# Low parts of the MLP weights: half of them by an adding transfer instead of a DVE subtraction

## The chip, the core and the metric

The kernel runs on one core of a Trainium2 chip, as one launch. The metric is device microseconds (us) from start to end of that launch. The engines are PE (TensorE matmul, with PEld for its weight loads), DVE (VectorE), ACT (ScalarE), POOL (GpSimd) and SP (SyncE, which here only issues transfers); transfers of all queues run on the core's 16 DMA engines.

## What is computed

A decoder trunk of two layers over 256 tokens of width 2048, all in float32: layer 0 mixes with a gated DeltaNet, layer 1 with differential attention; each layer then has an MLP and a gated per-layer embedding (PLE), and a final RMSNorm closes. The change touches only the MLP, whose hidden width is 8192, and the buffers of the final norm.

```python
hn = rmsnorm(h, norm_mlp[i])
h = h + jnp.square(jax.nn.relu(hn @ mlp_w1[i])) @ mlp_w2[i]
gate = jax.nn.sigmoid(rmsnorm(h, norm_ple[i]) @ ple_w_gate[i])
h = h + (p[i] @ ple_w_proj[i]) * gate
```

## The kernel before

Every large product is done in a split form. Both operands are float32; each is written as a high part, rounded to the matmul type fp32r, and a low part, which is the raw value minus the high part. Three matmuls then replace one: high by high, high by low, low by high (L150 to L152 in `g2`, L166 to L168 in `g1`).

Weights come in by `chunk` (L117): SP loads 1 MB of raw weights into a tile `raw` of 128 partitions by 2048 float32 (L122; three buffers, pool `wraw`). The tile is split into two halves of 1024 columns. For each half ACT casts `whi` from `raw` (L131), and DVE writes `wlo` = `raw` - `whi` (L132). `whi` and `wlo` have three buffers each (pool `whl`), so a cast for half n+3 waits until PE has read half n. A half feeds 24 matmuls of 256 columns in `g2` or 12 matmuls of 512 columns in `g1`.

The MLP (`mlp`, L553 on) works through the hidden width in four quarters q. `first(q)` multiplies the normalised input by `mlp_w1` with `g2`: four blocks `nb` of 512 columns with four chunks each. At the end of a block ACT applies relu (L574), DVE squares (L575), ACT casts the high part `hidh` (L578) and DVE subtracts for the low part `hidl` (L579). `second(q)` multiplies by `mlp_w2` with `g1`, again four blocks of four chunks, and DVE adds the result to the stream `h` (L587). The order is first 0, first 1, second 0, first 2, second 1, first 3, second 2, second 3. Each stage has 16 chunks, so one MLP has 128 chunks, and the two MLPs have 256 chunks, 512 halves.

Each engine works through its own queue in order, and a queue stands still while its next instruction waits. The scheduler of the language sets the order of instructions on each queue when the program is built; semaphores tie the queues together. A new load of `raw` waits until all readers of that buffer's earlier contents are done.

The layer's tiles come from a pool `ffn0` or `ffn1` with two buffers for each name: `hidh`, `hidl`, `relu` and others. `ple` loads its `p` tiles from POOL's queue (L600). `final` (L723) loads `final_norm` into a `hidl` buffer from POOL's queue (L725) and writes its results into eight tiles `y`.

Of the kernel before, what the change touches and what calls it, by code (L numbers as in the profile page):

```python
# [10 lines left out]
F32 = mybir.dt.float32  # L11
F32R = mybir.dt.float32r
AF = mybir.ActivationFunctionType
ALU = mybir.AluOpType
AX = mybir.AxisListType

P = 128
D = 2048
T = 256
NT = T // P  # L20
KD = D // P
# [16 lines left out]
class Trunk:  # L38
# [75 lines left out]
        self.w_gdn = self.cols[:, 112:113]  # L114
        self.w_sub = self.cols[:, 113:115]

    def chunk(self, src, kn, cols):  # L117

        nc = self.nc
        raw = self.wraw.tile([P, 2048], F32, name="raw")  # L120
        size = kn * cols
        nc.sync.dma_start(out=raw[:, :size].rearrange("p (k n) -> p k n", k=kn),  # L122
                          in_=src.rearrange("(k p) n -> p k n", p=P))
        res = []
        step = 1024 // cols
        for k0 in range(0, kn, step):
            kk = min(step, kn - k0)
            sl = raw[:, k0 * cols:(k0 + kk) * cols]
            hi = self.whl.tile([P, 1024], F32R, name="whi")[:, :kk * cols]
            lo = self.whl.tile([P, 1024], F32R, name="wlo")[:, :kk * cols]  # L130
            nc.scalar.copy(hi, sl)  # L131
            nc.vector.tensor_tensor(lo, sl, hi.bitcast(F32), ALU.subtract)  # L132
            res.append((hi.rearrange("p (k n) -> p k n", k=kk),
                        lo.rearrange("p (k n) -> p k n", k=kk), k0, kk))
        return res

    def g2(self, x, w, nk, c0, cols, kn):

        nc = self.nc
        xh, xl = x  # L140
        nct = cols // P
        banks = [self.bank() for _ in range((nct + 1) // 2)]
        for kb in range(0, nk, kn):
            for hi, lo, k0, kk in self.chunk(w[kb * P:(kb + kn) * P, c0:c0 + cols], kn, cols):
                for k in range(kk):
                    kt = kb + k0 + k
                    for ct in range(nct):
                        o = banks[ct // 2][:, (ct % 2) * T:(ct % 2) * T + T]
                        cs = slice(ct * P, ct * P + P)
                        nc.tensor.matmul(o, hi[:, k, cs], xh[:, kt], start=kt == 0 and ct % 2 == 0, stop=False, skip_group_check=True)  # L150
                        nc.tensor.matmul(o, hi[:, k, cs], xl[:, kt], start=False, stop=False, skip_group_check=True)  # L151
                        nc.tensor.matmul(o, lo[:, k, cs], xh[:, kt], start=False, stop=kt == nk - 1, skip_group_check=True)  # L152
        return banks

    def g1(self, x, w, nk, c0, kn=4, pool=None):

        nc = self.nc
        xh, xl = x
        banks = [self.bank(512, pool) for _ in range(NT)]
        for kb in range(0, nk, kn):  # L160
            for hi, lo, k0, kk in self.chunk(w[kb * P:(kb + kn) * P, c0:c0 + 512], kn, 512):
                for k in range(kk):
                    kt = kb + k0 + k
                    for t in range(NT):
                        ts = slice(t * P, t * P + P)
                        nc.tensor.matmul(banks[t], xh[:, kt, ts], hi[:, k], start=kt == 0, stop=False)  # L166
                        nc.tensor.matmul(banks[t], xh[:, kt, ts], lo[:, k], start=False, stop=False)  # L167
                        nc.tensor.matmul(banks[t], xl[:, kt, ts], hi[:, k], start=False, stop=kt == nk - 1)  # L168
        return banks
# [388 lines left out]
    def mlp(self, h, layer, w, pool):  # L558
        nc, d = self.nc, self.d
        w1, w2 = d["mlp_w1"][layer], d["mlp_w2"][layer]  # L560
        self.transposed(h, [(self.xa, w)])
        r = self.rstd(h)
        r2 = self.small.tile([P, NT], F32, name="r2")
        nc.vector.tensor_tensor(r2, r, r, ALU.mult)

        def first(q):
            hh = pool.tile([P, KD, T], F32R, name="hidh")
            hl = pool.tile([P, KD, T], F32R, name="hidl")
            for nb in range(4):
                for b, bk in enumerate(self.g2(self.xa, w1, KD, q * D + nb * 512, 512, 4)):  # L570
                    k = nb * 4 + 2 * b
                    a = pool.tile([P, 512], F32, name="relu")
                    s = pool.tile([P, 512], F32, name="relu2")
                    nc.scalar.activation(a, bk, AF.Relu)  # L574
                    nc.vector.tensor_tensor(s, a, a, ALU.mult)  # L575
                    fh = hh[:, k:k + 2].rearrange("p a b -> p (a b)")
                    fl = hl[:, k:k + 2].rearrange("p a b -> p (a b)")
                    nc.scalar.copy(fh, s)  # L578
                    nc.vector.tensor_tensor(fl, s, fh.bitcast(F32), ALU.subtract)  # L579
            return hh, hl  # L580

        def second(q, hid):
            for nb in range(4):
                bk = self.g1(hid, w2[q * D:(q + 1) * D], KD, nb * 512)
                for t in range(NT):
                    s = h[t][nb]
                    nc.vector.scalar_tensor_tensor(s, bk[t], r2[:, t:t + 1], s, ALU.mult, ALU.add)  # L587

        prev = first(0)
        for q in range(1, 4):  # L590
            cur = first(q)
            second(q - 1, prev)
            prev = cur
        second(3, prev)

    def ple(self, h, layer, w, pool):
# [125 lines left out]
    def final(self, h, pool):  # L722
        nc = self.nc  # L723
        fw = pool.tile([P, D], F32, name="hidl")
        nc.gpsimd.dma_start(out=fw, in_=self.d["final_norm"].partition_broadcast(P))  # L725
        y = [[pool.tile([P, 512], F32, name=f"y{t}{b}", bufs=1) for b in range(4)] for t in range(NT)]
        for b in range(4):
            for t in range(NT):
                nc.vector.tensor_tensor(y[t][b], h[t][b], fw[:, b * 512:(b + 1) * 512], ALU.mult)
        r = self.rstd(h)  # L730
        for t in range(NT):
            for b in range(4):
                if b % 2 == 0:
                    nc.scalar.activation(y[t][b], y[t][b], AF.Copy, scale=r[:, t:t + 1])
                else:
                    nc.vector.tensor_scalar(y[t][b], y[t][b], r[:, t:t + 1], None, ALU.mult)
                nc.sync.dma_start(out=self.out[0, t * P:(t + 1) * P, b * 512:(b + 1) * 512], in_=y[t][b])
# [55 lines left out]
```

## Time and profile before

| what | value |
|---|---|
| median of the two runs | 2951.43 us (2949.67 and 2953.2) |
| the profiled execution: its time | 2951.79 us |
| the profiled execution: its span in the profile | 2950.0 us |
| PE busy | 2909.7 us, 99% of the span |
| DVE busy | 1782.8 us, 60% |
| ACT busy | 1451.8 us, 49% |
| POOL busy | 60.4 us, 2% |
| DMA, mean rate over the span | 179 GB/s |

The page gives busy times of one execution. Busy time of PE is the union of matmuls that overlap, so the time that a matmul costs is the distance between the starts of two neighbours, not its own duration. An arrow in a row of idle time names what the engine waited for. The share of DMA is the mean busy share of the 16 engines.

### The profile page before, as it was taken

Reading aid. Unit: us, or ns where it says so; the run is one execution under the profiler, and the core shown is the slowest. Engines: PE = TensorE matmul, PEld = TensorE weight load, DVE = VectorE, ACT = ScalarE, POOL = GpSimd, SP = SyncE. Lnnn points to the kernel's source line nnn. Section 1 sums busy time; section 2 is a strip of 40 time slices with the busy share of each in tenths; the row PEclk is TensorE's granted clock in tenths of the full one; section 3 lists DMA queues with packets and bytes.
Section 4 is the critical chain, followed back from the end, with each engine's and each line's share of the span. In section 5 each row is a group of like instructions: output and inputs, shape, how many; then the busy total and the mean of one; then the engine's idle time right before and its main releaser. Section 6 shows DMA issues by size and latency. Waiting matters only on the chain.

```text
span 2950.0 us, 44777 instructions
## 1 busy us (share of the span) xinstructions
PE 2909.7 (99%) x18730; PEld 2626.2 (89%) x18730; DVE 1782.8 (60%) x2324; ACT 1451.8 (49%) x1947; POOL 60.4 (2%) x64
## 2 busy tenths in 40 slices
PE   8999999999999999999999999999999999999998
PEld 8989889988988998989988889987899899898886
DVE  7879766666666555555555565567555555555565
ACT  5655555545545443444434553367544444344454
POOL 1011000000000000000000000000000000000000
PEclk9999999999999999999999999999999999999999
DMA  6654544455445665655565556654566565556654
GB/s 200 207 168 140 175 161 138 149 175 161 133 143 182 194 196 190 188 194 189 186 198 189 178 170 198 191 166 144 183 192 197 189 192 192 188 186 198 202 172 155
DMA packets 289595, 527.19 MB, mean 179 GB/s; under 512 B 25966, under 2 KB 44560, under 8 KB 289264
## 3 DMA queue, kind: packets, MB, share of 16 engines
q1 hardware_dynamic: 288160, 521.77, 55.3%
q8 instruction: 147, 2.41, 0.3%
q0 software_dynamic: 816, 2.03, 0.2%
q10 hardware_dynamic: 416, 0.53, 0.1%
q14 instruction: 56, 0.46, 0.0%
HBM read 520.03 MB, written 4.26 MB: 178 GB/s over the span
## 4 chain that ended last, share of the span: by engine, by line
PE 93%; DVE 4%; ACT 2%; DMA 0%; issue 0%; POOL 0%; ACTq 0%; DVEq 0%
PE accb L166 16%; PE accb L167 16%; PE accb L168 16%; PE accb L151 13%; PE accb L152 13%; PE accb L150 13%; PE misb L429 2%; DVE wlo L132 1%; ACT whi L131 1%; PE misb L434 1%; PE misb L412 0%; PE misb L444 0%; PE misb L193 0%; PE misb L421 0%; DMA h<-x 0%
## 5 line engine op out<-in xcount | busy, mean ns | idle before, releaser
L132 DVE TENSOR_TENSOR wlo<-raw,whi 128x1024 fp32r<-128x1024 f32 x970 | 1190.1, 1228 | 985.0 <-ACT whi L131 983.6
L131 ACT CAST whi<-raw 128x1024 fp32r<-128x1024 f32 x970 | 1019.2, 1051 | 1296.8 <-PE accb L168 677.5
L150 PE MATMUL accb<-xha,whi 128*128 128x256 f32 x3344 | 939.4, 281 | 0.8 <-ACT whi L131 0.8
L151 PE MATMUL accb<-xla,whi 128*128 128x256 f32 x3344 | 937.6, 280 | 1.6 <-DVE xla L198 1.6
L152 PE MATMUL accb<-xha,wlo 128*128 128x256 f32 x3344 | 936.9, 280 | 0.5 <-DVE wlo L132 0.5
L152 PEld LDWEIGHTS accb<-xha,wlo 128*128 128x128 f32 x3344 | 633.2, 189 | 0.7 <-DVE wlo L132 0.7
L151 PEld LDWEIGHTS accb<-xla,whi 128*128 128x128 f32 x3344 | 629.7, 188 | 2.4 <-DVE xla L198 2.2
L150 PEld LDWEIGHTS accb<-xha,whi 128*128 128x128 f32 x3344 | 630.4, 189 | 1.4 <-ACT whi L131 1.0
L168 PE MATMUL accb<-whi,hidl 128*128 128x512 f32 x1024 | 398.5, 389 | 0.0
L167 PE MATMUL accb<-wlo,hidh 128*128 128x512 f32 x1024 | 398.5, 389 | 0.0
L166 PE MATMUL accb<-whi,hidh 128*128 128x512 f32 x1024 | 398.5, 389 | 0.0
L166 PE MATMUL accb<-whi,xha 128*128 128x512 f32 x640 | 254.2, 398 | 1.2 <-ACT xha L197 1.2
L167 PE MATMUL accb<-wlo,xha 128*128 128x512 f32 x640 | 252.8, 395 | 0.1
L168 PE MATMUL accb<-whi,xla 128*128 128x512 f32 x640 | 251.9, 394 | 0.0
L168 PEld LDWEIGHTS accb<-whi,hidl 128*128 128x128 f32 x1024 | 192.3, 188 | 40.1
L166 PEld LDWEIGHTS accb<-whi,hidh 128*128 128x128 f32 x1024 | 192.3, 188 | 39.9
L167 PEld LDWEIGHTS accb<-wlo,hidh 128*128 128x128 f32 x1024 | 192.3, 188 | 39.1
L166 PEld LDWEIGHTS accb<-whi,xha 128*128 128x128 f32 x640 | 120.4, 188 | 26.2 <-ACT xha L197 2.5
L167 PEld LDWEIGHTS accb<-wlo,xha 128*128 128x128 f32 x640 | 120.5, 188 | 25.0 <-DVE wlo L132 1.4
L168 PEld LDWEIGHTS accb<-whi,xla 128*128 128x128 f32 x640 | 120.3, 188 | 24.2
L166 PE MATMUL accb<-whi,oh 128*128 128x512 f32 x256 | 101.1, 395 | 0.8 <-ACT oh L469 0.8
L167 PE MATMUL accb<-wlo,oh 128*128 128x512 f32 x256 | 101.1, 395 | 0.0
(276 smaller groups left out, 2616.5 us busy)
## 6 DMA issues: line engine op xcount, KB each, us to landing
raw<-mlp_w SPq DMA_DIRECT2D x256, 1024.0 KB, 5.2
raw<-gdn_w_in SPq DMA_DIRECT2D x97, 1024.0 KB, 5.1
raw<-gdn_w_out SPq DMA_DIRECT2D x32, 1024.0 KB, 5.0
raw<-ple_w_gate SPq DMA_DIRECT2D x32, 1024.0 KB, 5.0
raw<-w_kv SPq DMA_DIRECT2D x32, 1024.0 KB, 5.2
raw<-diff_w_q SPq DMA_DIRECT2D x16, 1024.0 KB, 5.0
raw<-diff_w_o SPq DMA_DIRECT2D x16, 1024.0 KB, 5.0
gcb<-gcd SPq DMA_DIRECT2D x16, 256.0 KB, 4.3
```

The costliest lines, as they stand in the source:

```text
L131: nc.scalar.copy(hi, sl)
L132: nc.vector.tensor_tensor(lo, sl, hi.bitcast(F32), ALU.subtract)
L150: nc.tensor.matmul(o, hi[:, k, cs], xh[:, kt], start=kt == 0 and ct % 2 == 0, stop=False, skip_group_check=True)
L151: nc.tensor.matmul(o, hi[:, k, cs], xl[:, kt], start=False, stop=False, skip_group_check=True)
L152: nc.tensor.matmul(o, lo[:, k, cs], xh[:, kt], start=False, stop=kt == nk - 1, skip_group_check=True)
L166: nc.tensor.matmul(banks[t], xh[:, kt, ts], hi[:, k], start=kt == 0, stop=False)
L167: nc.tensor.matmul(banks[t], xh[:, kt, ts], lo[:, k], start=False, stop=False)
L168: nc.tensor.matmul(banks[t], xl[:, kt, ts], hi[:, k], start=False, stop=kt == nk - 1)
L429: nc.tensor.matmul(ps[:, h * P:(h + 1) * P], NTt[:, 2 * h + c], X[:, h * P:(h + 1) * P], start=True, stop=True)
L434: nc.tensor.matmul(ps[:, h * P:(h + 1) * P], UB[:, 2 * h + c], X[:, h * P:(h + 1) * P], start=True, stop=True)
```

## The change

`chunk` gets an argument `pool`, which only the MLP's calls of `g2` and `g1` pass on. With it, the second half of every chunk (`k0` not 0) gets its low part in another way: ACT writes `dlo` = -`raw`, rounded to fp32r, into a tile of four new buffers, which is the negated high part; then a transfer from POOL's queue adds the raw half to it in place, from one place in SBUF to another. DVE's subtraction for that half is gone. The first half of every chunk stays as it was. All products outside the MLP stay as they were. The four buffers take 16 KB of each partition; `final` now keeps its results in one `hidh` buffer of the pool instead of eight tiles of its own.

```diff
@@ chunk
             hi = self.whl.tile([P, 1024], F32R, name="whi")[:, :kk * cols]
-            lo = self.whl.tile([P, 1024], F32R, name="wlo")[:, :kk * cols]
             nc.scalar.copy(hi, sl)
-            nc.vector.tensor_tensor(lo, sl, hi.bitcast(F32), ALU.subtract)
+            if pool and k0:
+                lo = pool.tile([P, 1024], F32R, name="dlo", bufs=4)[:, :kk * cols]
+                nc.scalar.activation(lo, sl, AF.Copy, scale=-1.0)
+                nc.gpsimd.dma_start(out=lo.bitcast(F32), in_=sl, accum_op=ALU.add)
+            else:
+                lo = self.whl.tile([P, 1024], F32R, name="wlo")[:, :kk * cols]
+                nc.vector.tensor_tensor(lo, sl, hi.bitcast(F32), ALU.subtract)
@@ mlp
-                for b, bk in enumerate(self.g2(self.xa, w1, KD, q * D + nb * 512, 512, 4)):
+                for b, bk in enumerate(self.g2(self.xa, w1, KD, q * D + nb * 512, 512, 4, pool)):
-                bk = self.g1(hid, w2[q * D:(q + 1) * D], KD, nb * 512)
+                bk = self.g1(hid, w2[q * D:(q + 1) * D], KD, nb * 512, wpool=pool)
@@ final
-        y = [[pool.tile([P, 512], F32, name=f"y{t}{b}", bufs=1) for b in range(4)] for t in range(NT)]
+        ys = pool.tile([P, 2 * D], F32, name="hidh")
+        y = [[ys[:, (4 * t + b) * 512:(4 * t + b + 1) * 512] for b in range(4)] for t in range(NT)]
```

The scheduler also moves instructions. On ACT in the first MLP, stage first 0, the queue before has for each chunk its two casts, chunk after chunk; the numbers of `raw` tell the chunks apart.

```order
L131 CAST whi_9311<-raw_9309 128x1024
L578 CAST hidh_9001<-relu2_9238 128x512
L574 ACTIVATE relu_9243<-accb_9004 128x512
L131 CAST whi_9315<-raw_9309 128x1024
L578 CAST hidh_9001<-relu2_9244 128x512
L131 CAST whi_9369<-raw_9367 128x1024
L131 CAST whi_9373<-raw_9367 128x1024
L131 CAST whi_9427<-raw_9425 128x1024
```

The same place of ACT's queue in the changed kernel, a little further on (consecutive chunks are raw_9873, raw_9932, raw_10007, raw_10066):

```order
L131 CAST whi_9875<-raw_9873 128x1024
L131 CAST whi_9879<-raw_9873 128x1024
L134 ACTIVATE dlo_10015<-raw_10007 128x1024
L131 CAST whi_9934<-raw_9932 128x1024
L131 CAST whi_9938<-raw_9932 128x1024
L134 ACTIVATE dlo_10074<-raw_10066 128x1024
L131 CAST whi_10009<-raw_10007 128x1024
L131 CAST whi_10013<-raw_10007 128x1024
```

The negated copy of a chunk stands ahead of the casts of the chunk before it: dlo_10015 of raw_10007 comes before both casts of raw_9932, so it is the first reader of its chunk.

On POOL, in the second MLP, the queue had between the loads of `p` (L606 is L600 of before) and the end only the load of `final_norm`; now the adding transfers stand there, and the load of `final_norm` is among them.

```order
L606 DMA p_26091<-p 128x256
L606 DMA p_26092<-p 128x256
L135 DMA dlo<-raw 128x1024 x115
L731 DMA hidl<-final_norm 128x2048
L135 DMA dlo<-raw 128x1024 x13
```

Thirteen adding transfers now stand behind the load of `final_norm`, which waits for a `hidl` buffer. SP's queue keeps its order.

At the entry of the first MLP the queue of ACT was, before (`xha` is the high part of the MLP's input):

```order
L131 CAST whi<-raw 128x1024 x2
L197 ACTIVATE xha<-misb,cols 128x256 x4
L178 ACTIVATE junk,ss<-h_81 128x512
L197 ACTIVATE xha<-misb,cols 128x256 x3
```

and is now, at the same place:

```order
L131 CAST whi<-raw 128x1024
L134 ACTIVATE dlo<-raw 128x1024
L203 ACTIVATE xha<-misb,cols 128x256 x7
L184 ACTIVATE junk,ss<-h_81 128x512
```

A negated copy has taken the place of the second cast ahead of `xha`; that cast follows later.

## Rows read from the trace of the kernel before

**Rows 1.** The page: span, engines, and the two costliest groups (line, engine, tiles, count | busy, mean ns).
```profile
span 2950.0 us, 44777 instructions
PE 2909.7 (99%) x18730; PEld 2626.2 (89%) x18730; DVE 1782.8 (60%) x2324; ACT 1451.8 (49%) x1947; POOL 60.4 (2%) x64
...
L132 DVE TENSOR_TENSOR wlo<-raw,whi 128x1024 fp32r<-128x1024 f32 x970 | 1190.1, 1228 | 985.0 <-ACT whi L131 983.6
L131 ACT CAST whi<-raw 128x1024 fp32r<-128x1024 f32 x970 | 1019.2, 1051 | 1296.8 <-PE accb L168 677.5
```

**Rows 2.** Busy time by stretch, stages of both MLPs (PEclk: granted clock; then DMA share, GB/s).
```profile
931.50:1102.90 171.40, 171.40 (x1515) 171.40 (x1514) 97.07 (x99) 82.75 (x97) 0.00 (x0) 1.00 0.61 191
1102.90:1189.90 87.00, 87.00 (x386) 72.07 (x385) 45.86 (x43) 35.34 (x36) 0.00 (x0) 1.00 0.60 194
1189.90:1280.40 90.50, 90.50 (x770) 90.48 (x769) 47.85 (x46) 40.44 (x45) 0.00 (x0) 1.00 0.59 187
...
sum 1401.00, PE 1401.00 PEld 1281.41 DVE 749.78 ACT 614.98 POOL 0.54; mean PE 116.75 PEld 106.78 DVE 62.48 ACT 51.25 POOL 0.04
```

**Rows 3.** Waits, first MLP, 931.5 to 1632 us (us in total, times, longest).
```profile
DVE wlo L132 <- ACT whi L131: 317.1, 254, 1.6
ACT whi L131 <- PE accb L168: 199.7, 124, 1.7
ACT whi L131 <- PE accb L151: 154.6, 98, 1.8
```

**Rows 4.** DMA of one stage, second 0, 1102 to 1190 us.
```profile
DMA packets 8452, 16.84 MB, mean 191 GB/s; under 512 B 256, under 2 KB 256, under 8 KB 8448
q1 hardware_dynamic: 8448, 16.78, 59.2%
raw<-mlp_w SPq DMA_DIRECT2D x17, 1024.0 KB, 5.0
```

**Rows 5.** DMA around the load of final_norm, 2746 to 2754 us.
```profile
q1 hardware_dynamic: 624, 1.25, 49.7%
q0 software_dynamic: 144, 1.05, 31.0%
raw<-mlp_w SPq DMA_DIRECT2D x2, 1024.0 KB, 5.1
hidl<-final_norm POOLq DMA_DIRECT2D x1, 1024.0 KB, 7.0
```

**Rows 6.** The tile raw over the whole run: its landing times.
```profile
DMA to landing us min/median/max: 3.7/5.1/9.5
```

**Rows 7.** ACT in first 2, in order of time (start, us, engine, ... [idle before]).
```profile
1209.79 1.05 ACT L131 CAST whi<-raw 128x1024 fp32r<-128x1024 f32 x1 [1.78 <-PE accb L151]
1212.02 0.60 ACT L574 ACTIVATE relu<-accb 128x512 f32<-128x512 f32 x1 [1.19 <-PE accb L152]
...
1213.57 0.62 ACT L578 CAST hidh<-relu 128x512 fp32r<-128x512 f32 x1
```

**Rows 8.** PE and DVE at the end of the last product, in order of time.
```profile
2934.27 0.39 PE L166 MATMUL misb<-whi,ph 128*128 128x512 f32 x1
2936.76 0.39 PE L168 MATMUL misb<-whi,pl 128*128 128x512 f32 x1
2936.58 1.37 DVE L619 TENSOR_TENSOR gate<-gate,misb 128x512 f32<-128x512 f32 x2 [5.24 <-PE misb L168]
```

**Rows 9.** POOL in order of time: loads of p and of final_norm.
```profile
924.82 1.13 POOL L600 DMA_DIRECT2D p<-p  x2 [145.61 <-PE misb L193]
2746.96 0.54 POOL L725 DMA_DIRECT2D hidl<-final_norm  x1 [619.51 <-DVE h L587]
```

**Rows 10.** ACT and PE at the entry of the first MLP, in order of time.
```profile
924.29 1.05 ACT L131 CAST whi<-raw 128x1024 fp32r<-128x1024 f32 x1 [1.73 <-PE accb L168]
925.24 1.56 ACT L197 ACTIVATE xha<-misb,cols 128x256 fp32r<-128x256 f32 x4
927.04 0.39 PE L151 MATMUL accb<-xla,whi 128*128 128x256 f32 x1 [0.78 <-DVE xla L198]
```

More of the change, by code (lines that the diff above doesn't have):

```diff
@@ L115, in constants2, with chunk @@
         self.w_sub = self.cols[:, 113:115]
-    def chunk(self, src, kn, cols):
+    def chunk(self, src, kn, cols, pool=None):
         nc = self.nc
@@ L135, in chunk, with g2 @@
         return res
-    def g2(self, x, w, nk, c0, cols, kn):
+    def g2(self, x, w, nk, c0, cols, kn, wpool=None):
         nc = self.nc
@@ L143, in g2 @@
         for kb in range(0, nk, kn):
-            for hi, lo, k0, kk in self.chunk(w[kb * P:(kb + kn) * P, c0:c0 + cols], kn, cols):
+            for hi, lo, k0, kk in self.chunk(w[kb * P:(kb + kn) * P, c0:c0 + cols], kn, cols, wpool):
                 for k in range(kk):
@@ L153, in g2, with g1 @@
         return banks
-    def g1(self, x, w, nk, c0, kn=4, pool=None):
+    def g1(self, x, w, nk, c0, kn=4, pool=None, wpool=None):
         nc = self.nc
@@ L160, in g1 @@
         for kb in range(0, nk, kn):
-            for hi, lo, k0, kk in self.chunk(w[kb * P:(kb + kn) * P, c0:c0 + 512], kn, 512):
+            for hi, lo, k0, kk in self.chunk(w[kb * P:(kb + kn) * P, c0:c0 + 512], kn, 512, wpool):
                 for k in range(kk):
```

## The prediction

> **What bounds the kernel now.** I read the page first: PE is busy for 2909.7 of 2950.0 us, DVE for 1782.8 and ACT for 1451.8 [rows 1]. An average over stages decides nothing, so I read the MLP's stages next: in both MLPs together PE is busy for 1401.00 of 1401.00 us, at a granted clock of 1.00, with DVE at 749.78 and ACT at 614.98 [rows 2]. The waits of that stretch say the same from the other side: DVE waits for ACT's cast (317.1 us), ACT waits for PE to give back a `whi` buffer (199.7 and 154.6 us), and no row has PE waiting for DVE [rows 3]. So the chain there is matmul after matmul, and the engine that the change relieves is two steps away from it. The tempo is one chunk per 87.00 / 16 = 5.44 us in `second` and about 5.66 us in first 2 (90.50 / 16) [rows 2]; a half takes 2.72 us.
>
> **What the change removes.** 256 subtractions of 1228 ns each [rows 1], 314 us of DVE work, all of it hidden under PE. Its worth on the end is nothing: no wait of PE goes with it.
>
> **What it adds, step by step.**
>
> ACT: 256 copies of 128x1024. The nearest row is the cast of the same shape, 1051 ns [rows 1], so 269 us. In a chunk of `second` ACT then has 3 x 1.05 = 3.15 us of 5.44; at the end of a block in `first` two relus (0.60) and two casts to `hidh` (0.62) are added once in four chunks [rows 7]. It fits, and PE covers it.
>
> POOL: 256 issues. A POOL issue takes 0.54 us [rows 9], 138 us over 1401: covered.
>
> The transfers: 256 times 512 KB, SBUF to SBUF, with an add. No row shows one, so I bound its cost from both sides. In one stage the loads of `raw` take 59.2% of the engines' time [rows 4]: 0.592 x 5.44 = 3.22 us of each engine per chunk, and 2.22 us are free. A transfer of 512 KB is 32 KB for each of 16 engines. The loads' packets of 2 KB take 0.592 x 88 x 16 / 8448 = 0.099 us each [rows 4]; the packets of `final_norm`, about 8 KB, take 0.310 x 8 x 16 / 144 = 0.276 us [rows 5]. At these prices 32 KB moved once cost 4 x 0.276 = 1.10 us or 16 x 0.099 = 1.58 us. If an add must read both its source and its target through the same engine, it is twice that, 2.20 or 3.16 us. The rows of the new transfer are 4 KB long, a third of the way from the one packet to the other: 1.26 us for one pass, 2.53 us for two. One pass gives 3.22 + 1.26 = 4.48 of 5.44 us, hidden. Two give 5.75, which is over by 0.31 us. The free 2.22 us are the point from which it decides.
>
> I take the hidden case. The nearest row is 1 MB that POOL's queue moved at the start of second 3, twice the new transfer's bytes: within 8 us, the two loads of `raw` beside it landed in 5.1 us, as without it, and it landed itself in 7.0 us [rows 5, 6]. Also, loads at 59.2% of the time carry 191 GB/s on average [rows 4], while the 8 us around `final_norm` carried (1.25 + 1.05) MB, 287 GB/s, at 49.7 + 31.0 = 80.7% [rows 5].
>
> The Trainium skill speaks against it: in "Collectives: The Full Stack", section "The bandwidth ceiling: the fold count and why AG ≠ RS ≠ AR", an add inside a transfer costs no time of its own, but it needs two source reads on the same read ring and so halves the rate. By that rule the second pass is the case, and the time is that of the first rival below. No row here shows an adding transfer, so no trace yet agrees or disagrees.
>
> **Latency of the new chain.** The order puts the negated copy of chunk c+2 behind the second cast of chunk c. That cast starts when PE has left half 2c-2; the copy ends about 2.1 us later, and PE reaches the second half of chunk c+2 six halves after it left half 2c-2, at 16.3 us. The slack is 14.2 us; a POOL-issued 1 MB landed in 7.0 us [rows 5]. With four `dlo` buffers the target is free by then. So the landing alone does not stall PE.
>
> **The new wait, and who is queued behind it.** The copy is now the first reader of its `raw` tile, and ACT's queue has the two casts of the chunk before behind it. The load of chunk c+3 starts when the second cast of chunk c is done; after the landing come copy, cast, cast of chunk c+2, and its last cast lets the next load go. This ring may take two chunks, 10.88 us. It holds 3.15 us of ACT, so a landing of up to 7.7 us costs nothing. The landing is 5.1 us in the median and 9.5 us at its longest [rows 6]; one pass beside it makes it 5.1 + 1.26 = 6.4 us, two passes 7.6 us. In the hidden case 1.3 us are left.
>
> **Moved.** On POOL thirteen transfers stand behind the load of `final_norm`, which waited until DVE's add to `h` at 2746.96 us [rows 9], the end of second 2. The first of the thirteen belongs to the fourth chunk of second 3; its copy is due some 5 us later. No stall. At the entry of each MLP a copy takes the place of a cast ahead of `xha`, where PE does wait (0.78 us) [rows 10]; the cast was over by 925.34 us, and the copy may have to wait for the pool's memory until about 924.8 us, when `p` went out [rows 9], so it ends at about 925.9: 0.6 us later, 1.2 us for both. The results of `final` in `hidh` cost nothing, since that buffer was given back by second 2.
>
> **Sum.** The profiled execution's own time is 2951.79 us, span 2950.0 and 1.8 around it; that is 0.4 us above the median of the runs. Removed 0, entry +1.2, the rest hidden: 2953.0.
>
> A bound for what I can't explain: first 0 and 1 hold 1515 matmuls in 171.40 us, 0.113 us each; first 2 holds 770 in 90.50, 0.118 us, with the same code and no wait [rows 2]. Four stages of 768 at 0.0044 us are 13.5 us that another layout could win or lose.
>
> **The rivals.**
>
> *The DMA engines become the bound (slower).* An add in two passes needs 5.75 us per chunk at the middle price: +0.31 x 256 = +79 us, 3032 us. At the price of 2 KB packets it is 3.22 + 3.16 = 6.38: +0.94 x 256 = +241 us, 3194 us. For it: nothing in the kernel moves so many bytes per chunk now, and source and target are both in SBUF. Against: the row of `final_norm` [rows 5]. It decides at 2.22 us of engine time per transfer.
>
> *ACT's queue waits for its load (slower).* If landings stretch over 7.7 us for another reason than engine time, casts come late and, round the ring, loads too. At the longest landing of the trace, 9.5 us [rows 6], the ring takes 12.65 us, 6.33 per chunk: +0.89 x 256 = +228 us, 3181 us. For it: the copy waits where the cast had a landing long behind it. Against: the median landing leaves 2.6 us.
>
> *PE gets quicker with a quieter DVE (faster).* If the slow stages fell to the tempo of first 0, 13.5 us would go: 2939 us; over 2% it would take 59 us of 1401. Against: in the last microseconds, where DVE had been idle for 5.24 us, eleven distances between 512-column matmuls take 2.49 us, 0.226 each [rows 8], the same as 87.00 / 384 = 0.227 in `second`, with DVE busy for 45.86 of 87.00 us [rows 2]. The tempo does not hang on DVE.
>
> **Chances and range.** Hidden: 0.60. DMA engines the bound: 0.25. ACT's queue: 0.11. Quicker PE: 0.04. The prediction is the likeliest, 2953 us, with a range of its own of 2936 to 2969 (the 13.5 us each way and a little for the entry). Over all cases the range is 2936 to 3195: it takes in the two-pass case at both prices and the ACT case, and leaves out longer adds and a faster PE, about 0.12. Two per cent, about what a measurement of this kernel can tell from no change, is 59 us. Within it lie the hidden case and the cheapest part of the two-pass case, 0.62; slower are the rest of the two rivals, 0.34; faster 0.04.
>
> **What the profile after should show.** DVE's subtractions fall from 970 to 714 and DVE to about 1469 us; ACT rises to about 1721, POOL to about 199. The software queue carries 134 MB more. If I am right, PE stays busy for all of both MLPs, landings of `raw` are 5 to 7 us, and the queue's share is below 41% of the MLP's time. If the first rival holds, the DMA share in the MLP is above 95% and PE waits for `dlo` or for `whi`. If the second holds, the share stays under 90%, and ACT's largest wait is a copy for the landing of `raw`. What would make me wrong above all is the engine time of an add, which no row here shows.

## The result and the profile of the changed kernel

The changed kernel takes 3021.04 us in the median (3018.29 and 3023.79) against 2951.43: ratio 1.0239, 95% interval 1.0209 to 1.0268. It is 70 us slower. The forecast of 2953 us missed, and with it the case that was given 0.60. The range to 3195 held the time because it took in the two slower rivals.

The page of the changed kernel, the lines that answer to [rows 1]; behind the span and the engines stand two DMA queues (packets, MB, share), the chain that ended last by engine and by line, and two transfers with KB each and median us to landing:

```profile
span 3022.0 us, 45900 instructions
PE 2941.2 (97%) x18730; PEld 2626.7 (87%) x18730; DVE 1473.3 (49%) x2068; ACT 1667.8 (55%) x2203; POOL 282.9 (9%) x320
...
q1 hardware_dynamic: 288160, 521.77, 51.3%
q0 software_dynamic: 37680, 136.26, 23.7%
...
PE 54%; DMA 26%; DVE 7%; ACT 7%; issue 4%; POOL 0%; ACTq 0%; SPq 0%; DVEq 0%; POOLq 0%
DMA raw<-mlp_w 25%; PE accb L173 9%; PE accb L174 8%; PE accb L172 8%; PE accb L158 7%; PE accb L156 7%; PE accb L157 7%; DVE wlo L138 5%; ACT whi L131 4%; PE misb L435 2%; DMA dlo<-raw 1%; ACT relu L580 1%; PE misb L440 1%; PE misb L418 1%; PE misb L450 0%
...
raw<-mlp_w SPq DMA_DIRECT2D x256, 1024.0 KB, 7.9
dlo<-raw POOLq DMA_DIRECT2D x256, 512.0 KB, 6.7
```

DVE lost its 310 us, ACT gained 216, the software queue 134 MB. But the loads of `raw` now land in 7.9 us, and a quarter of the chain is their landing.

Where the 72 us between the two profiled spans lie, by the starts of PE's matmuls: the two MLPs hold all of it, 29.2 us in the first (707.9 before, 737.0 now) and 42.5 in the second (707.9, 750.4); the rest sums to 0.3. By stage, first MLP and second: first 0 with first 1 +12.9 and +15.2; second 0 +4.8 and +6.3; first 2 -0.1 and -0.4; second 1 +6.0 and +5.7; first 3 0.0 and +0.3; second 2 with second 3 +5.6 and +15.5. Stretches of the changed kernel, columns as in [rows 2]: second 0, first 2, second 1:

```profile
1115.70:1207.50 91.80, 89.28 (x386) 71.39 (x385) 26.62 (x27) 49.18 (x52) 13.94 (x16) 1.00 1.00 276
1207.50:1297.90 90.40, 89.64 (x769) 89.35 (x768) 28.11 (x30) 53.40 (x60) 13.94 (x16) 1.00 1.01 278
1297.90:1390.92 93.02, 90.08 (x387) 71.23 (x385) 26.83 (x28) 49.27 (x52) 13.93 (x16) 1.00 1.00 273
```

The share of the DMA engines (last but one) went from 0.60 to 1.00. A chunk now takes 5.74 us in second 0 and 5.65 in first 2. Where PE needed 5.44 before, time is lost; first 2 and 3, which needed 5.66, lose nothing on balance. DMA of second 0 (1116 to 1207 us), as in [rows 4]:

```profile
q1 hardware_dynamic: 8429, 16.75, 51.4%
q0 software_dynamic: 2288, 8.32, 48.3%
...
raw<-mlp_w SPq DMA_DIRECT2D x16, 1024.0 KB, 8.0
dlo<-raw POOLq DMA_DIRECT2D x16, 512.0 KB, 6.6
```

An adding packet takes 0.483 x 91 x 16 / 2288 = 0.307 us. A transfer has nine packets on each engine, so 2.77 us where the sum had taken 1.26. The loads' own part fell, from 3.22 us a chunk to 0.514 x 5.74 = 2.95. The sum, 5.72 us, fills the chunk; this reads like the first rival, engines with no time left. The chain of the same stage, in order of time (start, us, what), tells of something narrower:

```profile
1122.52 7.96 DMA raw<-mlp_w
...
1130.57 0.04 ACT dlo L134
...
1130.69 0.84 issue
1131.53 1.04 ACT whi L131
...
1132.60 1.24 DVE wlo L138
1133.84 0.02 SPq L123
...
1133.90 7.67 DMA raw<-mlp_w
```

A load lands; ACT makes the negated copy of that chunk, then casts the chunk before it; DVE subtracts there; this frees a buffer, and SP starts the next load. That is 7.96 + 3.42 = 11.38 us, and the order gives it two chunks: 5.69 us each. What SP waits for in the same stage (us in total, times, longest) shows a second chain of almost the same length:

```profile
SPq L123 <- DMA dlo<-raw: 73.2, 16, 6.3
SPq L123 <- DVE wlo L138: 10.1, 16, 1.1
```

The add is also a reader of `raw`. SP waits for it first, and for DVE's subtraction 0.63 us (10.1 / 16) longer. The experiments had to tell whether the engines' time or these chains set the tempo.

### The profile page after: what moved, and what is told of

Read it like the earlier page. It is cut to its first block, busy times and chain, and to the rows that moved or that the text cites. A ratio compares the mean times of both kernels' runs of the same rounds, so it can differ in the third digit from the quotient of the medians.

```text
span 3022.0 us, 45900 instructions
## 1 busy us (share of the span) xinstructions
PE 2941.2 (97%) x18730; PEld 2626.7 (87%) x18730; DVE 1473.3 (49%) x2068; ACT 1667.8 (55%) x2203; POOL 282.9 (9%) x320
## 3 DMA queue, kind: packets, MB, share of 16 engines
q8 instruction: 147, 2.41, 0.3%
## 4 chain that ended last, share of the span: by engine, by line
PE 54%; DMA 26%; DVE 7%; ACT 7%; issue 4%; POOL 0%; ACTq 0%; SPq 0%; DVEq 0%; POOLq 0%
DMA raw<-mlp_w 25%; PE accb L173 9%; PE accb L174 8%; PE accb L172 8%; PE accb L158 7%; PE accb L156 7%; PE accb L157 7%; DVE wlo L138 5%; ACT whi L131 4%; PE misb L435 2%; DMA dlo<-raw 1%; ACT relu L580 1%; PE misb L440 1%; PE misb L418 1%; PE misb L450 0%
## 5 line engine op out<-in xcount | busy, mean ns | idle before, releaser
L138 DVE TENSOR_TENSOR wlo<-raw,whi 128x1024 fp32r<-128x1024 f32 x714 | 876.2, 1229 | 1214.3 <-ACT whi L131 1213.0
L158 PE MATMUL accb<-xha,wlo 128*128 128x256 f32 x2320 | 654.5, 282 | 10.8 <-DVE wlo L138 10.7
L134 ACT ACTIVATE dlo<-raw 128x1024 fp32r<-128x1024 f32 x256 | 271.8, 1062 | 593.4 <-DMA raw<-mlp_w 589.7
L158 PEld LDWEIGHTS accb<-xha,wlo 128*128 128x128 f32 x2320 | 440.0, 190 | 15.6 <-DVE wlo L138 15.3
L135 POOL DMA_DIRECT2D dlo<-raw x256 | 223.1, 871 | 1236.4 <-ACT dlo L134 1043.0
L158 PE MATMUL accb<-xha,dlo 128*128 128x256 f32 x1024 | 285.3, 279 | 5.8 <-DMA dlo<-raw 5.8
L173 PE MATMUL accb<-wlo,hidh 128*128 128x512 f32 x512 | 207.4, 405 | 17.7 <-DVE wlo L138 17.2
L158 PEld LDWEIGHTS accb<-xha,dlo 128*128 128x128 f32 x1024 | 194.5, 190 | 6.2 <-DMA dlo<-raw 6.2
L173 PE MATMUL accb<-dlo,hidh 128*128 128x512 f32 x512 | 199.4, 389 | 0.0
L173 PEld LDWEIGHTS accb<-wlo,hidh 128*128 128x128 f32 x512 | 96.5, 189 | 58.3 <-DVE wlo L138 39.5
```

The costliest lines, as they stand in the source:

```text
L134: nc.scalar.activation(lo, sl, AF.Copy, scale=-1.0)
L135: nc.gpsimd.dma_start(out=lo.bitcast(F32), in_=sl, accum_op=ALU.add)
```

## Experiments

The expectations of the first eight runs weigh the engines' time for the adds (D, where a letter is used) against the queue and the ring of buffers (Q). Diffs are against the changed kernel. Ratios are to the kernel before, run on the same chip.

**The same transfers without the add.** The add is left out, so `dlo` holds the raw weights.

```diff
-                nc.gpsimd.dma_start(out=lo.bitcast(F32), in_=sl, accum_op=ALU.add)
+                nc.gpsimd.dma_start(out=lo.bitcast(F32), in_=sl)
```

> The change with the adding transfer turned into a plain copy of the same bytes on the same queue (no add, so the low part of the second halves is the raw weight: this part of the computation is wrong). Theory D (the 16 DMA engines are the bound in the MLP, because an add costs each engine two passes, 2.7 us of its time per 512 KB, where 2.2 us are free): a copy is one pass, 1.3 to 1.6 us, 3.2 + 1.5 = 4.7 of 5.44 us per chunk, so it hides and the time is 2950 to 2962 us; packets of the software queue take about half of their 0.30 us. Theory S (the software queue as such is slow, by issue or latency, whatever it carries): about 3020 us. Theory Q (ACT's queue stands behind the landing of raw, and the ring of loads is too short): between them, 2960 to 3020, as the landing is shorter by 1.3 us at most.

Measured: 2968.87 us, ratio 1.0051 (1.0034 to 1.0068). DMA of first 2, 1193.8 to 1284.3 us:

```profile
q1 hardware_dynamic: 8452, 16.78, 60.9%
q0 software_dynamic: 2322, 8.46, 22.9%
...
raw<-mlp_w SPq DMA_DIRECT2D x16, 1024.0 KB, 5.8
```

A copying packet takes 0.229 x 90.5 x 16 / 2322 = 0.143 us, less than half of the adding one. Loads land in 5.8 us, and second 0 takes 87.06 us, as before. So the add itself matters. The time still lies above the range of D (2962) and inside that of Q: in the trace, 6.0 and 4.4 us more than before lie in first 0 and 1 of the two MLPs. First 2 also kept its tempo (90.45 us) with DVE as idle as in the changed kernel, so the rival of a quieter DVE has nothing for it.

**The add on DVE, the copies on ACT.**

```diff
-                nc.gpsimd.dma_start(out=lo.bitcast(F32), in_=sl, accum_op=ALU.add)
+                nc.vector.tensor_tensor(lo, sl, lo.bitcast(F32), ALU.add)
```

> The change without the transfer: ACT still writes the negated copy, in the same place of its queue and in the same buffers, and DVE adds the raw half to it. Theory D: nothing is left on the DMA engines but the loads, so 2950 to 2956 us, and landings of raw at 5.1 us. Theory Q: the copy ahead of the casts still waits for the landing; if the order alone costs, the time stays above 2960 us.

Measured: 2957.3 us, ratio 1.0002 (0.9992 to 1.0011), loads landing in 5.2 us. ACT's 256 copies, their order ahead of the casts and the buffers cost nothing as long as loads land that early.

**Half the width**, and **every other chunk**: half the adds' bytes, by narrower rows and by fewer transfers.

```diff
-                nc.gpsimd.dma_start(out=lo.bitcast(F32), in_=sl, accum_op=ALU.add)
+                nc.gpsimd.dma_start(out=lo[:, :512].bitcast(F32), in_=sl[:, :512], accum_op=ALU.add)
+                nc.vector.tensor_tensor(lo[:, 512:], sl[:, 512:], lo[:, 512:].bitcast(F32), ALU.add)
```

> The adding transfer covers only 512 of the 1024 columns, DVE adds the raw weights to the other 512; as many transfers as before, half the bytes. Theory D: 3.2 + 1.4 = 4.6 of 5.44 us, hidden, 2950 to 2970 us. If the cost goes by transfer, not by bytes: 3000 to 3020 us.

```diff
-            if pool and k0:
+            if pool and k0 and self.turn():
```

(`turn` is true at every other call.)

> Only every second chunk of the MLP gives its second half to the transfer: 128 transfers in place of 256. Theory D: over two chunks 6.4 + 2.7 = 9.1 of 10.9 us, hidden on the average, 2950 to 2965 us. If each transfer stalls PE by itself, by its wait: half of the loss, about 2986 us.

Measured: 2971.5 us, 1.0058 (1.0043 to 1.0073), and 2956.16 us, 1.0007 (0.9996 to 1.0019). Loads landed in 5.9 and 5.2 us. In the stages after the entry half the bytes are all but hidden, whichever half; the half-width kernel kept 20 us, a little over its expected range. Its trace puts 8.5 and 8.2 of them into first 0 and 1 of the two MLPs and 3.7 into the last `second`.

**The adds for both halves of a chunk.**

```diff
-            if pool and k0:
+            if pool:
```

> Both halves of every chunk get their low part by transfer: 512 transfers. Theory D: 3.2 + 5.4 = 8.6 us per chunk in place of 5.54, 256 x 3.1 = 790 us over the kernel before, 3650 to 3850 us, with a DMA share near 1.0. With four buffers for two transfers per chunk the chain is also shorter in hand, so more is possible; less than 3600 us would speak against a bound by engine time.

Measured: one execution, 3639.49 us, a little under its expected range; 2.41 us for each further transfer ((3639 - 3021) / 256). That is near to an add's engine time, 2.77. But loads landed in 10.0 us and adds in 9.0, which lengthens every chain too, and the mean granted clock was 0.952 (0.992 in the changed kernel). This run can't tell engines from ring.

**Two plain copies in place of an add.** The second goes to a tile that nothing reads; the add is left out here too. (The tile `gate` shares the buffers of `relu` to make room.)

```diff
-                nc.gpsimd.dma_start(out=lo.bitcast(F32), in_=sl, accum_op=ALU.add)
+                nc.gpsimd.dma_start(out=lo.bitcast(F32), in_=sl)
+                two = pool.tile([P, 1024], F32, name="two")[:, :kk * cols]
+                nc.gpsimd.dma_start(out=two, in_=sl)
```

> Two plain copies of the raw half per chunk in place of the adding transfer, one to the low part and one to a tile that nobody reads (no add, so the low part of the second halves is the raw weight: this part of the computation is wrong). One copy cost 9 packets of 0.143 us per engine in the run before. Theory D (engine time is the bound, and an add is two passes): 3.2 + 2 x 1.29 = 5.8 us per chunk, as with the add, so 3005 to 3035 us and a DMA share near 1.0 in the MLP. If it is something about the add other than engine time (waiting inside the add, its longer chain): as with one copy, 2960 to 2975 us.

Measured: 3135.17 us, 1.0604 (1.0583 to 1.0624), far above what was expected, at a DMA share of 0.95 (1230 to 1290 us, in the first MLP). By engine time it should have been as the add. What lasted longer was a buffer's hold: load 8.0, then copies that landed 7.6 us after their issue. That fits a ring of three buffers, about 18 us for three chunks of 6.2 (first 2 took 99.4 us). A piece of its chain is such a ring: a load of 9.26 us from 1239.55, POOL's issues, a copy landing in 6.96, and the next load at 1260.07. But no run took this kernel's ring away.

**A fourth buffer for `raw`.**

```diff
-        raw = self.wraw.tile([P, 2048], F32, name="raw")
+        if pool and self.fourth():
+            raw = pool.tile([P, 2048], F32, name="rawx", bufs=1)
+        else:
+            raw = self.wraw.tile([P, 2048], F32, name="raw")
```

(`fourth` is true at every fourth call; the tile `gate` shares the buffers of `relu` to make room.)

> Every fourth raw tile of the MLP comes from a buffer of its own, so that four chunks can be in flight instead of three (the gate tile of the PLE shares the buffers of relu to make room). Theory Q: the ring from cast to load to copy to cast gets a third longer, 16.3 us for a landing, and nearly all of the 70 us goes: 2951 to 2970 us. Theory D: the engines have the same work, 3.2 + 2.7 us per chunk, and the time stays at 3005 to 3025 us, with landings that get longer instead.

Measured: 3016.18 us, 1.0203 (1.0187 to 1.0218). By its expectation this spoke for the engines and against the ring. It doesn't, because the edit didn't reach the wait. ACT's queue of this kernel, consecutive chunks being raw_13017, raw_13052 and raw_13087:

```order
L141 ACTIVATE dlo_13095<-raw_13087 128x1024
L138 CAST whi_13019<-raw_13017 128x1024
L138 CAST whi_13023<-raw_13017 128x1024
```

The scheduler spent the new buffer on moving the copy: that of chunk c+2 now stands ahead of the casts of chunk c, where it stood ahead of those of c+1. The load still has to land, be copied and let two casts by within two chunks. Only the second chain, the add's hold on the buffer, was given a chunk more. SP's waits in second 0 (1116 to 1207 us) bear this out:

```profile
SPq L130 <- DVE wlo L145: 80.2, 16, 6.1
...
SPq L130 <- DMA dlo<-raw: 1.0, 2, 0.5
```

The adds (73.2 us in the changed kernel) hold SP up no more; the subtraction at the end of ACT's chain does. The stage still takes 94.2 us (91.8 in the changed kernel), so ACT's chain by itself is enough for the loss.

**The negated copies on POOL**, and **the same with four buffers for `raw`**.

```diff
-                nc.scalar.activation(lo, sl, AF.Copy, scale=-1.0)
+                nc.gpsimd.tensor_scalar(lo, sl, -1.0, None, ALU.mult)
```

> The negated copy is made by POOL instead of ACT, so that no cast on ACT stands behind the landing of a raw tile; the adding transfer stays. Theory Q: the casts are free of the wait and the time falls to 2950 to 2965 us. Theory D: engine time per chunk is unchanged, so 3010 to 3030 us.

> The negated copies on POOL again, with a fourth buffer for raw as in the earlier experiment. If what bound the kernel with the copies on POOL (3197 us) is the ring of the raw buffers, each held for load 7.6 + negation 2.8 + issue 1.2 + add 7.2, about 19 us, then four buffers allow a chunk every 4.7 us, the ring is no longer the bound, and the time falls to that of the changed kernel with four buffers or a little above: 3015 to 3050. If it is POOL itself or a slower transfer, 3170 to 3200.

Measured: 3196.83 us, 1.0832 (1.0792 to 1.0871), and with four buffers 2982.52 us, 1.0096 (1.0063 to 1.0128). Both missed. The first was to show whether ACT's queue is to blame and met another bound: a copy took POOL 2891 ns, and each buffer was held for the load, the copy, the issue and the add, some 19 us. The fourth buffer took 214 us away, so that was the ring. It then went below the changed kernel, which no theory of engine time allowed: the adds are all there. With four buffers, the DMA of second 0 (1113 to 1199 us), and a row of its waits:

```profile
q1 hardware_dynamic: 8475, 16.81, 54.1%
q0 software_dynamic: 2341, 8.54, 50.4%
...
raw<-mlp_w SPq DMA_DIRECT2D x12, 1024.0 KB, 9.9
```

```profile
ACT whi L138 <- PE accb L181: 49.1, 30, 1.7
```

The engines stand at over 104% and loads land later than in the changed kernel, but ACT waits only for PE to give back `whi`. The stage takes 87.08 us, against 87.06 before the change (89.3 in the second MLP).

**Four buffers for `raw`, three for `dlo`.** Fewer `dlo` buffers hold the copies back to where they stood in the changed kernel, and the fourth buffer goes to the load.

```diff
+            raw = pool.tile([P, 2048], F32, name="rawx", bufs=1)
...
-                lo = pool.tile([P, 1024], F32R, name="dlo", bufs=4)[:, :kk * cols]
+                lo = pool.tile([P, 1024], F32R, name="dlo", bufs=3)[:, :kk * cols]
```

> Four buffers for raw again, but three for dlo. In the earlier run with four raw buffers the scheduler used the fourth one to move the negated copy a chunk further ahead on ACT: the copy of chunk c+2 stood ahead of the casts of chunk c, so that a landing, the copy, two casts and a subtraction still had to fit into two chunks, as in the changed kernel. With three dlo buffers the copy of chunk c+2 stands ahead of the casts of chunk c+1, as in the changed kernel, and the load that it waits for has three chunks of time. ACT's queue as the bound (a landing of 8.0 plus some 3.4 us in two chunks gives 5.7 us a chunk): with three chunks a landing of up to 12.9 us is hidden, second falls back to 87 to 89 us, and the time to 2970 to 2990. The engines' time for the adds as the bound, whatever the order: second stays at 91 to 94 us, and the time is 3010 to 3020.

Measured: 2968.14 us, 1.0053 (1.0036 to 1.0070). Second 0, first 2 and second 1 of this kernel (columns as in [rows 2]), and the DMA of second 0:

```profile
1118.00:1204.00 86.00, 86.00 (x381) 71.23 (x380) 26.10 (x26) 49.83 (x51) 13.93 (x16) 1.00 1.04 293
1204.50:1294.90 90.40, 90.40 (x769) 90.38 (x768) 28.33 (x30) 55.33 (x61) 13.94 (x16) 1.00 1.01 275
1294.97:1382.01 87.04, 87.04 (x387) 72.06 (x385) 26.86 (x27) 49.00 (x52) 13.93 (x16) 1.00 1.04 289
```

```profile
q1 hardware_dynamic: 8442, 16.77, 53.1%
q0 software_dynamic: 2297, 8.36, 50.3%
...
raw<-mlp_w SPq DMA_DIRECT2D x12, 1024.0 KB, 7.8
dlo<-raw POOLq DMA_DIRECT2D x12, 512.0 KB, 7.2
```

The same adds at the same price (0.503 x 86 x 16 / 2297 = 0.301 us a packet), the same copies on ACT, the same landing of 7.8 us, and PE is busy without a gap. Over the whole run loads land in 10.0 us. Against the four-buffer kernel, which stayed at 1.0203, one number is changed. SP now waits 1.3 us for the subtraction where it waited 80.2; it waits for adds instead (72.3), and PE doesn't feel that. So engine time was not the bound of the changed kernel; the chain from landing to the next load was. Three `dlo` buffers without the fourth for `raw` were not run.

**The entry.** The half-width kernel and the one above, with DVE subtracting in the first four chunks of each MLP.

```diff
-            if pool and k0:
+            if pool and k0 and self.late():
```

(`late` is false for the first four chunks of each MLP.)

> The half-width kernel again, but the first four chunks of each MLP take their low parts from DVE's subtraction, as in the kernel before. The half-width kernel was some 20 us above the kernel before, and in its trace 8 us of that lie in the stretch first 0 and 1 of each MLP (185.6 and 185.4 us, against 177.1 and 177.1). If that rest is the entry, where the second and third adds are issued late because their negated copies stand behind the casts to xha, so that the raw buffers come free late: 2952 to 2960, and first 0 and 1 take 177 to 179 us each. If it is the traffic of the adds as such, wherever it runs: 2968 to 2973, and the stretches stay at 184 to 186 us.

> As the run with four raw and three dlo buffers, but the first four chunks of each MLP take their low parts from DVE's subtraction. If what is left above the kernel before in that run is the entry of the two MLPs: 2955 to 2968. If it is the adds' time on the DMA engines in the long stretches: no lower than the run without this, less 8 us at most.

Measured: 2957.42 us, 1.0011 (1.0001 to 1.0022), and 2957.87 us, 1.0022 (1.0013 to 1.0032). Both as expected for the entry: 14 us of the half-width kernel (0.0047) and 9 of the other (0.0031) lay there. In the last one the share in second 0 (1101 to 1187 us) is 105% and loads land in 11.0 us; it costs nothing. It is the best version that keeps every add but those four per MLP, and still no better than the kernel before, in which PE had no gap to give [rows 2].

## Why the prediction was wrong

*What bounds the kernel, what is removed.* Right. DVE's 256 subtractions went and nothing came back for them.

*The price of the adding transfer.* This is the term that failed, by a factor of two: 1.26 us of each engine were taken for it, by the row of `final_norm`, and it is 2.77. The failing choice was the nearest row: a plain load says nothing of an add. The bound for two passes, 2.53, was near. For a plain copy 1.26 would have been right (1.29). By rows of these runs an adding packet takes 0.301 to 0.307 us, a plain copy of the same shape 0.143, a ratio of 2.1. The Trainium skill's rule for the reduce step of a ring ("Collectives: The Full Stack", section "The bandwidth ceiling: the fold count and why AG ≠ RS ≠ AR"), that an add needs two reads and so halves the rate, agrees with that ratio. That a second read is the cause, no run here shows. Nor is the price a matter of collision: in 935.8 to 940.4 us of the changed kernel, where the adds ran with next to no load beside them, it is 0.722 x 4.6 x 16 / 176 = 0.302 us:

```profile
q0 software_dynamic: 176, 0.66, 72.2%
q1 hardware_dynamic: 6, 0.01, 0.6%
```

*The point from which it decides.* Wrong in kind. The text said 2.22 us of free engine time per chunk, and an add takes 2.77. Yet six kernels had shares of 1.00 to 1.05 in `second`, and the two with three `dlo` buffers lost nothing there (87.04 to 87.06 us in second 0 and 1 of both MLPs). The share adds up the packets' times, and over 1.00 some of these must overlap, so 1.00 is not the end. The loads' part was no constant either (2.95 us for the 3.22 of the sum), so the forecast 5.75 for two passes met the measured 5.72 by luck.

*ACT's queue.* This is the wait that decided, and it was in the text, as the second rival: copy ahead of the casts, two chunks for a landing, and the landing may be 7.7 us. Two things were amiss. The ring held 3.42 us beside the landing, not 3.15, since DVE's subtraction is the last reader (1.24) in place of a second cast; that makes the limit 10.88 - 3.42 = 7.46 us. And the text had itself worked out 7.6 us as the landing beside two passes, then kept the case separate, as something that needs "another reason than engine time". The add's engine time was reason enough: beside plain copies of the same bytes loads landed in 6.3 us over the run (the forecast for one pass was 6.4), beside the adds in 7.9, and the wait did the rest. The first rival's cause acted through the second rival's wait. Its size: (11.38 / 2 - 5.44) = 0.25 us for the 192 chunks outside first 2 and 3, 48 us; the step from the changed kernel to the one with the chain relaxed is 1.0239 - 1.0053 = 0.0186, 55 us. The other 7 us may be what the granted clock took, which fell after waits of PE in the second MLP (an estimate is at the end).

*The first rival's 3032 us.* Near the time by compensation, that is by luck. It charged 0.31 us to all 256 chunks, the 64 of first 2 and 3 included, which lost nothing on balance, and left out the entries.

*The signs.* Neither rival's set came out whole. The share of over 95% was the first's; ACT's largest wait, the copy for the landing of `raw`, was the second's. Neither set was fit to tell them apart, because a bound by latency can stand beside a full share.

*The entry.* 1.2 us were taken for both; four chunks of DVE subtractions per MLP gave back about 9 us by ratio (1.0053 to 1.0022). The working looked at the first copy alone. The second copy stands behind all sixteen products to `xha` on ACT, so its add is issued ten microseconds after the first. POOL and then PE in the changed kernel, in order of time:

```profile
925.88 0.96 POOL L135 DMA_DIRECT2D dlo<-raw  x1
935.81 0.88 POOL L135 DMA_DIRECT2D dlo<-raw  x1 [8.97 <-ACT dlo L134]
```

```profile
940.27 0.58 PE L158 MATMUL accb<-xha,dlo 128*128 128x256 f32 x1 [2.61 <-DMA dlo<-raw]
```

The slack of 14.2 us is that of the steady state; here PE stands before the half 1.9 us after the issue and gets it 4.5 us after.

*The load of `final_norm`.* "No stall" was wrong in the changed kernel: PE has a gap of 4.55 us at 2830.70, behind a cast behind a copy that waited 8.37 us for its load. The 1 MB of `final_norm` was issued at 2812.85 into engines that were full, and that load of `raw`, issued 1.4 us after it, landed after 14.30 us. The four-buffer kernel has a gap of 4.86 us, 16 us after the same issue. That `final_norm` is the cause was not tried.

*POOL.* An adding issue takes 0.87 us, not 0.54; still covered.

*First 2 and 3.* Their slower matmuls, 0.118 us against 0.113, stand in most kernels run here, but they are not fixed. In first 2 of the changed kernel they take 0.118 us up to a wait of PE at 1265.21 us (0.76) and 0.113 from there on; in the half-width kernel with DVE at the entry, first 2 of the first MLP took 88.16 us for 90.45, at 0.113 from a wait at 1194.27 us (0.62) on. Stretches of the changed kernel (two) and of the other:

```profile
1207.52:1260.00 52.48, 52.48 (x447) 52.48 (x446) 16.47 (x18) 30.57 (x35) 7.84 (x9) 1.00 1.00 272
1270.00:1297.80 27.80, 27.80 (x247) 27.73 (x246) 8.70 (x10) 16.74 (x20) 4.36 (x5) 1.00 1.04 289
1200.00:1275.00 75.00, 75.00 (x664) 75.00 (x664) 34.41 (x40) 50.17 (x55) 12.22 (x14) 1.00 0.91 247
```

So in first 2 and 3 the changed kernel paid for some of its waits with quicker matmuls, and a part of the 13.5 us in the prediction's bound can be won (2.3 us in the other kernel). What sets the tempo is still open. So is the two-copy kernel's bound, and whether the engines or the ring hold the kernel with 512 adds. Of what is left in the last kernel (0.0022, some 6 us), its trace puts 1.9 us into the two entries and 2.9 into second 2 and 3 of the second MLP.

## What to carry to other kernels

When a transfer is added beside others, work out not only whether the DMA engines have time for it but how much later the other landings come, and then look for the instruction on an in-order queue that waits for such a landing ahead of work that PE needs; its slack, with every reader of the buffer counted, is the limit. A buffer more helps only if the scheduler doesn't spend it on moving the waiting instruction further ahead: read the order before trusting such an experiment. Price an adding transfer as two plain ones (2.1 here), and look at a stage's entry by itself, since the slack of the steady state isn't there yet.

## What the runs showed of the hardware

- An adding SBUF-to-SBUF transfer of 512 KB takes 2.7 to 2.8 us of each DMA engine, a plain one 1.29 (0.143 x 9); its issue takes POOL 0.87 us, that of the plain one 0.53.
- The mean share of the DMA engines can stand at 1.04 or 1.05 over a whole stage while nothing is late; the landings tell more (8 to 11 us then, against 5).
- After PE's gap of 2.61 us at the entry the granted clock fell. In the changed kernel, busy time from 940 to 944 us and from 944 to 950 (the column ahead of the DMA share is the granted clock):

```profile
940.00:944.00 4.00, 3.73 (x19) 3.73 (x20) 0.54 (x1) 0.00 (x0) 0.44 (x1) 0.57 1.05 198
944.00:950.00 6.00, 6.00 (x55) 6.00 (x55) 1.23 (x1) 1.76 (x2) 0.00 (x0) 1.00 1.02 306
```

  0.57 means most of those 4 us at the lower level of 1.2 GHz: 19 matmuls where the next 6 us hold 55. At the later pace the 19 would have taken 2.1 us in place of 3.7, so by this estimate 1.6 us more were lost after the gap of 2.6. In the second MLP the clock fell again after waits of PE: of 3.15 us at the entry, of 1.10 and 0.76 close together, of 2.21 and 0.76, and of 4.55 and 0.75. The last three:

```profile
2190.00:2203.00 13.00, 11.14 (x81) 10.74 (x81) 5.04 (x6) 8.11 (x11) 1.73 (x2) 0.87 1.00 280
2255.00:2268.00 13.00, 10.03 (x73) 9.63 (x72) 4.88 (x6) 8.25 (x11) 1.74 (x2) 0.87 0.79 212
2829.00:2841.00 12.00, 9.55 (x29) 7.40 (x30) 3.87 (x4) 6.94 (x8) 1.78 (x3) 0.72 0.82 181
```

  By an estimate they took 0.13 x 13 + 0.13 x 13 + 0.28 x 12 = 6.7 us. In the MLPs of the kernel before it stood at 1.00.
